# Half of the down projection's width by seven half-size products, in five chunks of the second MLP, with the left operand 64 bytes further on

## The chip, the cores and the metric

The kernel runs on one core of a Trainium2 chip. The metric is the time of one execution on the device in microseconds. The engines are called as in the profile: PE (TensorE, matmuls), PEld (its loads of the stationary operand), DVE (VectorE), ACT (ScalarE), POOL (GpSimd) and SP (SyncE, which issues most DMAs).

## The reference, cut to what matters

The network has two layers over 512 tokens of width 1024. Each layer is a mixer with a normalization and then this MLP with hidden width 4096, also with a residual and a normalization. All is float32.

```python
def sq_relu_mlp(h, w_up, w_down):
    return jnp.square(jax.nn.relu(h @ w_up)) @ w_down

        h = layer_norm(DN_ALPHA * h + sq_relu_mlp(h, mlp_w_up[layer], mlp_w_down[layer]),
                       ln_g[layer, 1], ln_b[layer, 1])
```

## The kernel before

**Three passes.** Each float32 operand is split into a high part (a cast to the matmul type, on ACT) and a low part (the raw value minus the high part, on DVE). A product is high x high, high x low and low x high, so three matmuls for each block of 128 of the contraction. `split` and `wload` do this: they write `wh`/`wl` (weights), `w2h`/`w2l` (half as large), and `hidden` writes `hh`/`hl`.

**Chunks.** `mlp` goes through the hidden width in eight chunks of 512. A chunk's hidden values lie in `hh` and `hl` (128 partitions, four blocks of 512 tokens). The loop over `c` has two halves, `n = 0, 1`. A half computes two blocks of the hidden values of chunk `c + 1` and then one half of the output columns of chunk `c`: `down(c, t, n, ...)` for four tiles `t` of 128 tokens. A `down` is 12 matmuls: left (stationary) operand `hh` or `hl`, moving operand `wh` or `wl` with 512 columns. `V.tensor_tensor` then adds the result from PSUM (`dn`) to the residual `res`.

**The up products.** The two blocks of hidden values are not made by eight half-size products but by seven (Winograd's form): `Pair.m1, m6, m2, m7, m5, m4, m3`, in this order on PE, 12 matmuls of 256 columns each. Their operands are sums of weight blocks, made by POOL (`up_load`: four sums into `sa` and `sb`) and split afterwards, and sums of activations (`TH`, `TL`). Results gather in three PSUM tiles: `a` (m1, m2), `b` (m6, m7, m4) and `d` (m5, m3). Between two products of one tile DVE reads it: `u2` after m6, `u3` after m7, `r22` after m5, so m7 waits for `u2`, m4 for `u3` and m3 for `r22`. `close` applies relu and square on ACT and splits into `hh` and `hl`.

**What sets the order.** Each engine runs its own list of instructions in order; a scheduler builds the lists from the program, and `behind(x, y)` puts x after y. The next pair of up weights is loaded while the current one is used. Raw weights take turns in four buffers (`wr`), `wh` and `wl` in five; a load waits until all readers of its buffer are done. `x0`, `pad2` and the like only set where the tiles lie in memory. `load_gb` loads a normalization's gain and bias.

## Time and profile before

| | |
|---|---|
| median of three runs | 1158.22 us (1158.12 to 1160.28) |
| the profiled execution | 1157.95 us |
| its span in the profile | 1156.2 us |
| busy: PE, DVE, ACT, POOL | 98%, 71%, 48%, 21% |
| DMA | 114.10 MB, mean 99 GB/s |

The profile shows one execution. Its span runs from the first to the last instruction, the execution's time holds 1.75 us more. A PE that is busy by the profile need not run at its peak, since the ends of matmuls are modelled; how far it is ahead is better read from the start times of successive matmuls.

### The profile page before, as it was taken

How to read it: one execution, taken by the hardware profiler on the slowest of the kernel's cores; microseconds unless marked ns; L12 is line 12 of the kernel's file. 1: busy time of each engine (PE TensorE's matmuls, PEld its weight loads, DVE VectorE, ACT ScalarE, POOL GpSimd, SP SyncE). 2: the span in 40 equal slices, each digit the busy share in tenths (PEclk: the TensorE clock that was granted, in tenths of full speed). 3: DMA queues.
4: the chain of work that ended last, by engine and by line, in shares of the span. 5: the costliest groups of instructions: out<-in, count | busy, mean ns of one | idle time of the engine just before them, and what ended most of it. 6: DMA issues, size and time to landing. Idle time of an engine off the chain costs nothing.

```text
span 1156.2 us, 19018 instructions
## 1 busy us (share of the span) xinstructions
PE 1135.4 (98%) x7542; PEld 1004.3 (87%) x7542; DVE 816.6 (71%) x1501; ACT 555.1 (48%) x1015; POOL 244.5 (21%) x177
## 2 busy tenths in 40 slices
PE   9999999999999999999999999999999999999997
PEld 9878789998998898998988887777988898989986
DVE  6667789667887676665665977877976665666657
ACT  6454743465584444444443345542644444444531
POOL 1112120011013242423420200000042422424203
PEclk9999999899999999999999999999999999999999
DMA  8522131304313243332334232202332332323312
GB/s 297 163 75 78 46 90 70 102 19 148 114 68 128 92 128 96 109 106 91 110 105 128 67 104 73 74 1 73 111 127 95 103 114 92 110 96 108 107 55 73
DMA packets 41257, 114.10 MB, mean 99 GB/s; under 512 B 11536, under 2 KB 12304, under 8 KB 41168
## 3 DMA queue, kind: packets, MB, share of 16 engines
q1 hardware_dynamic: 40736, 112.10, 29.7%
q8 instruction: 59, 0.97, 0.3%
q10 hardware_dynamic: 432, 0.79, 0.2%
q14 instruction: 30, 0.25, 0.1%
HBM read 109.46 MB, written 3.41 MB: 98 GB/s over the span
## 4 chain that ended last, share of the span: by engine, by line
PE 87%; DVE 6%; issue 3%; ACT 2%; POOL 1%; DMA 1%; SPq 0%; DVEq 0%; ACTq 0%; POOLq 0%
PE dn L69 30%; PE upb L69 9%; PE upd L69 6%; PE wo L69 6%; PE upa L69 6%; PE up L69 4%; PE projqMM L69 4%; PE kq L69 4%; PE proj_zMM L69 3%; PE v L69 3%; PE ssc L69 1%; PE ov L69 1%; PE ropeMM L69 1%; PE KM L69 1%; PE VM L69 1%
## 5 line engine op out<-in xcount | busy, mean ns | idle before, releaser
L108 ACT CAST wh<-wr 128x1024 fp32r<-128x1024 f32 (+1 forms) x124 | 130.5, 1053 | 213.8 <-PE dn L69 154.8
L109 DVE TENSOR_TENSOR wl<-wr,wh 128x1024 fp32r<-128x1024 f32 (+1 forms) x124 | 169.3, 1366 | 70.1 <-ACT wh L108 69.9
L69 PE MATMUL dn<-wh,hh 128*128 128x512 f32 (+1 forms) x516 | 200.2, 388 | 0.0
L69 PE MATMUL dn<-wh,hl 128*128 128x512 f32 (+1 forms) x516 | 200.1, 388 | 0.0
L69 PE MATMUL dn<-wl,hh 128*128 128x512 f32 (+1 forms) x516 | 200.1, 388 | 0.0
L1149 DVE TENSOR_TENSOR res<-res,dn 128x512 f32<-128x512 f32 (+1 forms) x121 | 82.1, 678 | 64.4 <-PE dn L69 64.3
L69 PEld LDWEIGHTS dn<-wh,hl 128*128 128x128 f32 x516 | 96.9, 188 | 19.9
L1058 POOL TENSOR_TENSOR sa<-wr 128x512 f32<-128x512 f32 x26 | 37.6, 1447 | 359.5 <-DMA wr<-in_up_dram 339.2
L69 PEld LDWEIGHTS dn<-wh,hh 128*128 128x128 f32 x516 | 96.9, 188 | 18.9
L69 PEld LDWEIGHTS dn<-wl,hh 128*128 128x128 f32 x516 | 96.9, 188 | 18.9
L825 POOL TENSOR_TENSOR rs<-rs,nhalf 128x1 f32<-128x1 f32 x16 | 13.2, 824 | 296.1 <-DVE rs L824 250.3
L69 PE MATMUL upb<-TH,wh 128*128 128x256 f32 x216 | 60.5, 280 | 0.7 <-DVE u L1107 0.6
L69 PE MATMUL upd<-XH,wh 128*128 128x256 f32 x216 | 59.9, 277 | 0.4 <-DVE r L1122 0.4
L69 PE MATMUL upa<-XL,wh 128*128 128x256 f32 x216 | 59.9, 277 | 0.0
L69 PE MATMUL upd<-XL,wh 128*128 128x256 f32 x216 | 59.8, 277 | 0.0
L69 PE MATMUL upa<-XH,wl 128*128 128x256 f32 x216 | 59.7, 277 | 0.0
L69 PE MATMUL upd<-XH,wl 128*128 128x256 f32 x216 | 59.7, 277 | 0.0
L69 PE MATMUL upb<-TH,wl 128*128 128x256 f32 x216 | 59.7, 276 | 0.0
L69 PE MATMUL upb<-TL,wh 128*128 128x256 f32 x216 | 59.7, 276 | 0.0
L1060 POOL TENSOR_TENSOR sa<-wr,wr 128x512 f32<-128x512 f32 x26 | 57.2, 2200 | 0.0
L1059 POOL TENSOR_TENSOR sb<-sa,wr 128x512 f32<-128x512 f32 x26 | 54.7, 2104 | 0.0
L975 ACT CAST wh<-wr 128x1024 fp32r<-128x1024 f32 x27 | 28.5, 1054 | 53.6 <-PE upa L69 53.6
(425 smaller groups left out, 3247.0 us busy)
## 6 DMA issues: line engine op xcount, KB each, us to landing
wr<-in_up_dram SPq DMA_DIRECT2D x64, 512.0 KB, 3.7
wr<-in_dn_dram SPq DMA_DIRECT2D x64, 512.0 KB, 3.8
wr<-in_wo_dram SPq DMA_DIRECT2D x16, 512.0 KB, 4.4
wr<-in_bw_dram SPq DMA_DIRECT2D x8, 512.0 KB, 4.2
wr<-in_wk_dram SPq DMA_DIRECT2D x6, 512.0 KB, 4.3
wr<-in_wq_dram SPq DMA_DIRECT2D x6, 512.0 KB, 3.5
wr<-in_wv_dram SPq DMA_DIRECT2D x6, 512.0 KB, 3.7
wr<-in_wz_dram SPq DMA_DIRECT2D x4, 520.0 KB, 3.9
```

The source lines that it names most:

```text
L69: return self.note(nc.tensor.matmul(*args, **kw))
L108: behind(A.copy(hi, raw), first_act)
L109: behind(V.tensor_sub(lo, raw, fr(hi)), first)
L825: G.tensor_tensor(rs, rs, nhalf[:, 0:1], op=ALU.pow)
L975: behind(A.copy(hi, raw), first_act)
L1058: e.tensor_tensor(sa[:, 0], raw[1][:, kA], raw[1][:, kB], op=ALU.add)
L1059: e.tensor_tensor(sb[:, 0], sa[:, 0], raw[0][:, kA], op=ALU.subtract)
L1060: e.tensor_tensor(sa[:, 1], raw[0][:, kA], raw[1][:, kA], op=ALU.subtract)
L1149: V.tensor_tensor(dst, dst, ps, op=ALU.add)
```

## The change

In chunks 2 to 6 of the second layer's MLP (`SD`) the left half of the output columns (0 to 511) is computed as before, but as two quarters of 256 columns each (`Quarter`). The right half (512 to 1023) is computed by seven products of half size (`Down`): the hidden chunk is cut into two halves of the contraction and two of the tokens, the weight into two halves of the contraction and two quarters of the columns. Four of the seven products take sums of hidden values as their left operand (`Sums`, written over `r` and split into `SH0`, `SL0`, `SH1`, `SL1`), four take sums of weights (`T1`, `T2`, `T3`, `T4`: `R1`'s first half, `R0`'s first half, and `tb`). All sums are made by POOL. Each product is 12 matmuls of 256 columns, and DVE adds each partial result to `res` when its product is done (`dns`, 2 x 256 columns).

In these chunks `hid_tiles` places `hh` and `hl` 16 elements (64 bytes) further on in their buffers. The buffers of the MLP are split up anew: `f4` has three instead of five, `r` has its own three, `tb` and the `S` tiles are new. The three PSUM banks of `mmt` get names, so that products can choose one. The gain and bias of the normalizations are loaded at other places. The evictions and splits of `Pair` get more `behind` conditions in these chunks.

```diff
+    def hid_tiles(dt, off=0):
+        both = (hid_pool[1].tile([P, 2112], dt, tag=n, name=nm(n)) for n in ("hh", "hl"))
+        return [h[:, off:off + 2048].rearrange("p (k t) -> p k t", k=4) for h in both]
...
-            return pool.tile(shape, F32, tag="f4", name=nm(n), bufs=5)
+            return pool.tile(shape, F32, tag="f4", name=nm(n), bufs=3)
+        def rt(shape, n):
+            return pool.tile(shape, F32, tag="r", name=nm(n), bufs=3)
...
-        def new_hid():
-            return hid_tiles(F32R)
+        def new_hid(c):
+            return hid_tiles(F32R, 16 if c in SD else 0)
...
+        SD = range(2, NC - 1) if layer == 1 else ()
+        nA, nB = slice(512, 768), slice(768, 1024)
+        class Quarter:
+            def __init__(self, c, m):
+                self.c, self.m = c, m
+                self.raw = columns(c, 0, m)
...
+            def tile(self, t, hid):
+                (hh, hl), (wh, wl) = hid, self.w
+                ps = smt("dnq")[:, 0:256]
+                for k in range(4):
+                    h, l = (x[:, k, t * P:(t + 1) * P] for x in hid)
+                    T.matmul(ps, h, wh[:, k, :], start=k == 0, stop=False)
+                    T.matmul(ps, h, wl[:, k, :], start=False, stop=False)
+                    T.matmul(ps, l, wh[:, k, :], start=False, stop=k == 3)
+                dst = res[:, t, self.m * 256:self.m * 256 + 256]
+                return V.tensor_tensor(dst, dst, ps, op=ALU.add)
+        def columns(c, n, m):
+            raw = wpool[0].tile([P, 4, 256], F32, tag="wr", name=nm("wr"), bufs=wpool[1])
+            for i in range(2):
+                SY.dma_start(raw[:, 2 * i:2 * i + 2, :], dn[layer, c, n, i][:, :, m * 256:m * 256 + 256])
+            return raw
+        class Down:
+            def __init__(self, c):
+                self.R0, self.R1 = (columns(c, 1, m) for m in range(2))
+                self.tb = tb("tb")
+            def sums(self, first):
+                b11, b21, b12, b22 = (r[:, i:i + 2, :] for r in (self.R0, self.R1) for i in (0, 2))
+                t3 = self.tb[:, 0:2, :]
+                behind(G.tensor_tensor(t3, b22, b12, op=ALU.subtract), first)
+                G.tensor_tensor(b12, b12, b11, op=ALU.subtract)
...
+                for rw, cl in zip(rows, cols):
+                    dst = res[:, rw.start // P:rw.stop // P, cl]
+                    self.out = V.tensor_tensor(dst, dst, ps, op=ALU.add)
+            def m1(self):
+                self.a = self.open(0)
+                self.product(self.a, self.hid, 0, tA, self.B11, True, False, [tA], [nA])
...
+        class Sums:
+            def __init__(self, r0, r1):
+                self.r = r0, r1
+                a11, a21, a12, a22 = (r[:, :, t] for r in self.r for t in (tA, tB))
+                G.tensor_tensor(a22, a21, a22, op=ALU.add)
+                G.tensor_tensor(a21, a11, a21, op=ALU.subtract)
+                G.tensor_tensor(a11, a22, a11, op=ALU.subtract)
+                self.last = G.tensor_tensor(a12, a12, a11, op=ALU.subtract)
...
+                    if fast and n == 0:
+                        d.split_0(p.u3_in, p.m2_out)
+                        d.sums_2()
...
+                elif n == 0:
+                    d.sums_3(nxt.sums)
+                    q.tile(0, hid)
+                    d.m1()
+                    nxt.split0(d.out, p.last)
+                    q.tile(1, hid)
+                    d.m2()
+                    nxt.split_b(d.out, p.last)
+                    o = q.tile(2, hid)
+                    d.m6()
+                    nxt.split_a(o, p.last)
+                    q.tile(3, hid)
+                    q = Quarter(c, 1)
+                else:
+                    d.m5()
...
-            if c == 1:
-                gb1 = load_gb(2 * layer + 1)
+            if c == NC - 2:
+                gb1 = load_gb(2 * layer + 1, *(f4([P, D], n) for n in ("lng", "lnb")))
```

How the lists move, at three places. First DVE, from the end of chunk 2 into the first half of chunk 3 of the second MLP, before. `wl` from `wr` with line 109 are the down slabs' splits, `dn` the down results; `u2`, `u3` and `r` with `upd` are the reads that m7, m4 and m3 wait for.

```order
L1149 TENSOR_TENSOR res_69<-res_69,dn_1530_10023 128x512
L109 TENSOR_TENSOR wl_1544_10094<-wr_1542_10091,wh_1543_10093 128x1024
L1149 TENSOR_TENSOR res_69<-res_69,dn_1533_10041 128x512
L109 TENSOR_TENSOR wl_1547_10100<-wr_1545_10097,wh_1546_10099 128x1024
L1107 TENSOR_TENSOR u2_1539_10085<-m1_1537_10070,upb_1538_10072 128x256
L1117 TENSOR_TENSOR u3_1549_10129<-m1_1537_10070,upb_1538_10072 128x256
L1122 TENSOR_TENSOR r_1548_10115<-u3_1549_10129,upd_1550_10131 128x256
L976 TENSOR_TENSOR wl_1557_10200<-wr_1551_10175,wh_1556_10199 128x1024
L1126 TENSOR_TENSOR r_1548_10115<-m1_1537_10070,upb_1538_10072 128x256
```

The same place after the change. `dnq` and `dns` are results of a quarter and of a product; `wr_1554` is the quarter, `wr_1555` is `R0`, split once as it was loaded and once (into `w2l`) when it holds T2.

```order
L1254 TENSOR_TENSOR res_69<-res_69,dns_1508_9831 128x2x256
L1120 TENSOR_TENSOR u2_1561_10228<-m1_1559_10213,upb_1560_10215 128x256
L988 TENSOR_TENSOR w2l_1563_10231<-wr_1538_10052,w2h_1562_10230 128x512
L988 TENSOR_TENSOR wl_1565_10235<-wr_1554_10188,wh_1564_10234 128x1024
L1130 TENSOR_TENSOR u3_1567_10264<-m1_1559_10213,upb_1560_10215 128x256
L988 TENSOR_TENSOR wl_1569_10267<-wr_1555_10191,wh_1568_10266 128x1024
L1135 TENSOR_TENSOR r_1566_10250<-u3_1567_10264,upd_1570_10271 128x256
L1293 TENSOR_TENSOR SL0_1574_10290<-r_1494_9733,SH0_1573_10289 128x1024
L988 TENSOR_TENSOR w2l_1572_10286<-wr_1555_10191,w2h_1571_10285 128x512
L1139 TENSOR_TENSOR r_1566_10250<-m1_1559_10213,upb_1560_10215 128x256
```

The splits no longer stand ahead of `u2` but between `u2`, `u3` and `r`, two ahead of `u3` and one ahead of the read that m3 waits for.

Second POOL, over the two pairs' sums around there, before: only `sa` and `sb`.

```order
L1058 TENSOR_TENSOR sa_1522_9981<-wr_1521_9978 128x512
L1060 TENSOR_TENSOR sa_1522_9981<-wr_1520_9977,wr_1521_9978 128x512
L1059 TENSOR_TENSOR sb_1523_9982<-sa_1522_9981,wr_1520_9977 128x512
L1061 TENSOR_TENSOR sb_1523_9982<-wr_1520_9977,sb_1523_9982 128x512
L1058 TENSOR_TENSOR sa_1553_10179<-wr_1552_10176 128x512
```

After: from the pair's sums of chunk 2's second half to those of chunk 3's first. Between them now stand the four sums of hidden values (`r`), two of `Down` (`tb`, and `wr_1556`, which becomes T1) and the one that writes T2 over `wr_1555`.

```order
L1074 TENSOR_TENSOR sb_1540_10056<-wr_1537_10051,sb_1540_10056 128x512
L1285 TENSOR_TENSOR r_1528_9979<-r_1494_9733,r_1528_9979 128x2x256
L1286 TENSOR_TENSOR r_1494_9733<-r_1494_9733 128x2x256
L1287 TENSOR_TENSOR r_1494_9733<-r_1528_9979,r_1494_9733 128x2x256
L1288 TENSOR_TENSOR r_1528_9979<-r_1528_9979,r_1494_9733 128x2x256
L1212 TENSOR_TENSOR tb_1557_10197<-wr_1556_10194 128x512
L1213 TENSOR_TENSOR wr_1556_10194<-wr_1556_10194,wr_1555_10191 128x512
L1217 TENSOR_TENSOR wr_1555_10191<-wr_1556_10194 128x512
L1071 TENSOR_TENSOR sa_1577_10327<-wr_1576_10324 128x512
```

Seven sums stand between the pairs where none stood; an eighth (into `tb`) follows the next pair.

Third PE, in a down tile of chunk 3 before, from the first slab's last block to the second slab's first (`wh` and `wl` moving, `hh` and `hl` left):

```order
L69 MATMUL dn_1564_10239<-wl_1544_10094,hh_1474_9661 128x512
L69 MATMUL dn_1564_10239<-wh_1543_10093,hl_1475_9662 128x512
L69 MATMUL dn_1564_10239<-wh_1546_10099,hh_1474_9661 128x512
L69 MATMUL dn_1564_10239<-wl_1547_10100,hh_1474_9661 128x512
L69 MATMUL dn_1564_10239<-wh_1546_10099,hl_1475_9662 128x512
```

The same chunk after, from the end of a quarter's tile into the first product.

```order
L69 MATMUL dnq_1579_10334<-wl_1565_10235,hh_1480_9669 128x256
L69 MATMUL dnq_1579_10334<-wh_1564_10234,hl_1481_9670 128x256
L69 MATMUL dns_1580_10348<-wh_1568_10266,hh_1480_9669 128x256
L69 MATMUL dns_1580_10348<-wl_1569_10267,hh_1480_9669 128x256
L69 MATMUL dns_1580_10348<-wh_1568_10266,hl_1481_9670 128x256
```

Every down matmul of these chunks is half as wide, and quarters and products take turns.

More of the change, by code (lines that the diff above doesn't have):

```diff
@@ L1043, in x_sums @@
                 split_copy(t, TH[:, i], TL[:, i])
+            for n in ("w2h", "w2l"):
+                pool.tile([P, 4, P], F32R, tag=n, name=nm(n), bufs=2)
             pool.tile([P, 40], F32, tag="pad3", name=nm("pad3"), bufs=1)
             xq["first"] = pool.tile([P, HT], F32R, tag="x0", name=nm("x0"), bufs=1)
-            pool.tile([P, 24], F32, tag="pad4", name=nm("pad4"), bufs=1)
             A.copy(xq["first"], fr(XH[:, 0, tA]))
@@ new lines, in mlp, with split @@
+        class Sums:
[6 more added lines that the diff above has]
+                self.last = G.tensor_tensor(a12, a12, a11, op=ALU.subtract)
+            def split(self, i, first, first_act):
+                hi, lo = (pool.tile([P, 2, 512], F32R, tag=f"S{n}{i}", name=nm(f"S{n}{i}"), bufs=1) for n in "HL")
+                behind(A.copy(hi, self.r[i]), first_act)
+                behind(V.tensor_sub(lo, self.r[i], fr(hi)), first)
+                return hi, lo
@@ L1184, in downs_last @@
             ln_out(*late_out)
+        gbt = [pool.tile([P, 2, 512], F32, tag=f"S{n}0", name=nm("gb"), bufs=1).rearrange("p a b -> p (a b)")
+               for n in "HL"]
+        for n in "HL":
+            pool.tile([P, 2, 512], F32, tag=f"S{n}1", name=nm("gb"), bufs=1)
+        if layer == 0:
+            gb0 = load_gb(0, *gbt)
         hid, nxt = ups_first()
@@ L1188, in mlp @@
         tables = rotary_tables(pool) if layer == 0 else None
+        sums = None
+        rs_ = {}
         for c in range(NC - 1):
-            later = new_hid()
+            later = new_hid(c + 1)
+            fast = c in SD
             for n in range(2):
@@ L1194, in mlp @@
                 early = c == n == 0
+                if fast and n == 0:
+                    q = Quarter(c, 0)
+                    d = Down(c)
+                    d.hid = hid
+                    d.sums(s_.last)
                 if p is None:
@@ L1285, in shared_kv @@
             split_copy(pt[:, 0:P], *[k[:, t * P:(t + 1) * P] for k in kTs])
-        mixTs = [[lt([P, 4, P], f"mix{n}{t}", 1, F32R) for n in "hl"] for t in range(NT)]
         nsink = lt([P, 12], "nsink", 1)
```

164 lines of the change are left out of this document (122 added, 42 removed).

## The prediction

> **What bounds the kernel now.** I read the page first, then the granted clock and the busy times by stretch, then the chain that ended last, and then the timeline of single engines in the second MLP.
>
> ```profile
> span 1156.2 us, 19018 instructions
> ...
> PE 1135.4 (98%) x7542; PEld 1004.3 (87%) x7542; DVE 816.6 (71%) x1501; ACT 555.1 (48%) x1015; POOL 244.5 (21%) x177
> ...
> PE 87%; DVE 6%; issue 3%; ACT 2%; POOL 1%; DMA 1%; SPq 0%; DVEq 0%; ACTq 0%; POOLq 0%
> ```
>
> TensorE (PE) carries 87% of the chain, so only fewer or faster matmuls make the kernel faster, as long as no other engine gets late. The stretches show whether one does in the chunks that change. The first row is one chunk of the second MLP (start and end, its length, then PE, PEld, DVE, ACT and POOL with counts, granted clock, DMA); the second is chunks 2 to 6 together.
>
> ```profile
> 961.14:1002.00 40.86, 40.86 (x265) 37.09 (x264) 25.51 (x32) 18.59 (x22) 14.28 (x8) 1.00 0.32 103
> 920.30:1126.05 205.75, 205.12 (x1321) 185.94 (x1320) 127.34 (x160) 92.42 (x109) 62.62 (x35) 1.00 0.30 98
> ```
>
> PE is busy without a gap, at a granted clock of 1.00. DVE has 15 us of a chunk to spare and POOL 26. The five chunks take 205.75 us where five of the first row would take 204.30, so 1.45 us of stalls lie in them. The chain has the pace of the matmuls, from a later half chunk:
>
> ```profile
> 1004.81 1.36 PE upb L69 x12
> ...
> 1012.97 10.89 PE dn L69 x48
> ```
>
> Twelve 256-wide matmuls take 1.36 us (0.1133 each) and 48 512-wide ones 10.89 (0.2269 each): a matmul of half the width costs exactly half.
>
> **Term 1, the products.** A chunk's down projection is now 96 matmuls 512 wide, 21.78 us. Afterwards its left half is the same work as 96 of 256, and its right half seven products of 12, so 84 of 256: 180 x 0.1133 = 20.40. The gain is one product, 1.36 us a chunk, 6.8 in five. Every one of these matmuls brings a weight load, 180 for 96; the up products have the same ratio, one load for each 256-wide matmul, at 0.1133.
>
> The Trainium skill (TensorE: Matmul & The Clock Gate, Back-to-back issue gap) gives 262 cycles for 256 columns and 518 for 512 at 2.4 GHz, an estimate of 0.1092 and 0.2158 us, a fixed part for each matmul. By it the change would gain 96 x 0.2158 - 180 x 0.1092 = 1.06 us a chunk, 5.3 in all; the trace, where 12 take 1.36 and 48 take 10.89, shows no such part in this stage.
>
> **Term 2, where the left operand lies.** Not every 256-wide matmul has that pace. These are the first and the last of 47 of the rotary projection, and the first and the last of the 24 that end the kernel:
>
> ```profile
> 656.51 0.37 PE L69 MATMUL ropeMM<-wh,XH 128*128 128x256 f32 x1
> ...
> 662.01 0.28 PE L69 MATMUL ropeMM<-wl,XH 128*128 128x256 f32 x1
> ...
> 1145.10 0.28 PE L69 MATMUL dn<-wh,hh 128*128 128x256 f32 x1
> ...
> 1147.85 0.28 PE L69 MATMUL dn<-wh,hl 128*128 128x256 f32 x1
> ```
>
> 5.50 us over 46 steps and 2.75 over 23 are 0.1196 both. In the built programs the next left operand starts, modulo 256 bytes, 0 bytes past the moving one in that last tile, 192 in the rotary projection, and 64 in the up products at 0.1133. The change puts the hidden tiles at 64, so I give their 132 matmuls a chunk the up products' pace (bounds 0 to 132 x 0.0063 = 0.83 us). The tiles of sums (SH, SL), left operand of four products, lie at 192: 48 x 0.0063 = 0.30 us a chunk (bounds 0 and 0.30). The row with the same distance is the nearest, so I take all of it: 1.5 us in five.
>
> **Term 3, VectorE and GpSimd.** The sums of the operands go to POOL, 16 a chunk instead of 8, and the splits into high and low parts to ACT and DVE. Times from one half chunk, POOL first, then DVE:
>
> ```profile
> 940.65 1.32 POOL L1058 TENSOR_TENSOR sa<-wr 128x512 f32<-128x512 f32 x1 [14.69 <-DMA wr<-in_up_dram]
> 941.93 2.30 POOL L1060 TENSOR_TENSOR sa<-wr,wr 128x512 f32<-128x512 f32 x1
> ```
>
> ```profile
> 941.80 1.25 DVE L109 TENSOR_TENSOR wl<-wr,wh 128x1024 fp32r<-128x1024 f32 x1 [1.76 <-ACT wh L108]
> 942.98 0.68 DVE L1149 TENSOR_TENSOR res<-res,dn 128x512 f32<-128x512 f32 x1
> 943.57 1.74 DVE L109 TENSOR_TENSOR wl<-wr,wh 128x1024 fp32r<-128x1024 f32 x1
> ...
> 949.23 1.22 DVE L976 TENSOR_TENSOR wl<-wr,wh 128x1024 fp32r<-128x1024 f32 x1
> 950.36 0.41 DVE L1126 TENSOR_TENSOR r<-m,upb 128x256 f32<-128x256 f32 x1
> ```
>
> A sum takes 1.32 us (1.28 from start to start). With a DVE split beside it 2.30, about 1.0 more, and the split at 943.57 takes 1.74, since that sum ends at 944.23. The add at 942.98, which reads PSUM, keeps its 0.68. So splits and sums take turns; adds from PSUM do not join. Back to back they alternate, and the one that waits nearly doubles:
>
> ```profile
> 842.87 2.29 POOL L1060 TENSOR_TENSOR sa<-wr,wr 128x512 f32<-128x512 f32 x1
> ```
>
> ```profile
> 841.66 2.34 DVE L976 TENSOR_TENSOR wl<-wr,wh 128x1024 fp32r<-128x1024 f32 x1
> 843.92 1.80 DVE L976 TENSOR_TENSOR w2l<-wr,w2h 128x512 fp32r<-128x512 f32 x1
> ```
>
> The turns of a chunk, before: 12 splits of 1024 at 1.13 (949.23 to 950.36), 2 of 512 at 0.68, 8 sums at 1.28, 25.2 us of 40.86. After: 15 at 1.13 (six for the pairs, two of hidden, two quarters, three of Down, two of Sums), 3 at 0.68, 16 sums at 1.28: 39.5 us. The matmuls of the chunk then take 40.86 - 1.36 = 39.5. **The turns fill the chunk**, and what counts is where they run late.
>
> ```profile
> L976 DVE TENSOR_TENSOR w2l<-wr,w2h 128x512 fp32r<-128x512 f32 x2 | 1.4, 684 | 0.0
> ```
>
> DVE itself has room: 19.0 us of splits, 18 adds of 256 at 0.41 and 7 of 512 at 0.68 make 31.1 of 39.5.
>
> Time zero of the walk is the end of a chunk's second row of up products. Rows for it, PE and then DVE:
>
> ```profile
> 951.57 10.89 PE dn L69 x48
> ```
>
> ```profile
> 955.50 1.22 DVE L983 TENSOR_TENSOR hl<-r,hh 128x1024 fp32r<-128x1024 f32 x1 [0.47 <-ACT hh L982]
> ```
>
> The split of the hidden part (hl) ends 955.50 + 1.22 - 951.57 = 5.15 us after zero; it now meets the next pair's last sum, 1.0 more, 6.15. Only then may Sums overwrite r. POOL's queue holds six sums from there (four of Sums, two of Down), 7.7 us, and DVE's five splits in turn with them (A11/A12, sb, sa, A22, quarter) push them by 4 x 1.0 + 0.6: they end at 18.45. The down products of that half take 8 x 1.36 = 10.88, so this is 7.6 into the next half. The split of R0, behind it, ends at 8.7 and the add of r22 behind that at 9.1. Product m3 writes the bank that r22 reads, and is due after six products, at 8.16. I take **0.9 us in chunks 3 to 6**, 3.6 in all; chunk 2 follows a chunk without these sums. Bounds: 0, if hl goes first, and 2.0, with one more exchange of 1.0. Behind r22 wait the splits of SL0 and T2, two adds and the evictions, which have the whole down part (9.5 us) as cover.
>
> **Term 4, an old stall.** One wait of this kind is in the trace, at the start of chunk 2:
>
> ```profile
> 920.23 0.31 DVE wl L109
> ...
> 924.73 0.42 DVE u L1107
> ...
> 925.19 1.68 PE upb L69 x12
> 926.87 1.41 PE upd L69 x12
> ```
>
> Two slab splits wait for sums, the add of u2 behind them comes late, and PE waits. In the new order no slab split stands ahead of u2, so I count 1.3 of the 1.45 us as gained (bounds 0 and 1.45).
>
> **At nothing.** DMAs of the down weights double in number for the same bytes; a tile lands 3.8 us after its issue (row below), R1, the last, some 3 us ahead of its first sum by the walk, and with that cover gone a load costs up to those 3.8 us. The gain and bias loads pass SP's queue elsewhere; in the second MLP they land over 20 us ahead of the last normalization. In the first up products of both layers other splits change places while DVE is full (27.99 of 28.00 us): bounds -1 and +1.
>
> ```profile
> wr<-in_dn_dram SPq DMA_DIRECT2D x64, 512.0 KB, 3.8
> ```
>
> ```profile
> 820.00:848.00 28.00, 27.89 (x195) 25.47 (x194) 27.99 (x30) 18.57 (x34) 7.01 (x4) 1.00 0.44 141
> ```
>
> **The sum.** -6.8 + 1.5 + 3.6 - 1.3 = -3.0 us. The profiled execution took 1157.95 (its span 1156.2 and 1.75 around it), so 1154.95; the median of the runs is 0.27 higher, so **1155.2**. A measurement of this kernel tells about 0.2%, 2.3 us, from no change.
>
> **Rivals.**
> - *The turns fit.* hl goes ahead of the pair's sums and r22 is in time. For it: DVE's 8.4 us to spare. Against: the sum of turns, 39.5 of 39.5. Without term 3: 1151.6.
> - *The backlog grows.* After the late r22 the adds behind SL0 and T2 end about 3.1 us after the first half's up products, hl about 7.3 after, and then come two splits, two adds and a sum of POOL: the split of sb ends 11.6 after, where m6 of the next half is due at 9.52 + 1.36 = 10.9. 0.7 more in four chunks: 1158.0, no change.
> - *The pace does not recover* (slower). After the wait at 925 each product took 1.41 us instead of 1.36, until the 512-wide matmuls. The new chunks have none, so from the first wait in chunk 3 on all 348 matmuls could run at 0.1175: 348 x 0.0042 x 4 = 5.8 us, 1161.0. Against: other 256-wide products kept 1.36.
> - *The 64 bytes do nothing*, and the hidden tiles run at the last tile's 0.1196: 0.83 x 5 = 4.2 us, 1159.4.
>
> **How the numbers follow.** Forecast 0.36 (own range 1153 to 1157.5), turns fit 0.17, backlog 0.20, pace 0.17, no use of the 64 bytes 0.10. Faster than 1155.9: two thirds of the forecast, all of the second, a little of the third, 0.44. Slower than 1160.5: the fourth and the edges of the third and fifth, 0.22. The rest, 0.34, lies between. The range, 1150.8 to 1161.5, takes in the second and the fourth and the bounds of terms 2 and 3 that they hold.
>
> **What would show it.** Chunks 2 to 6 should take 202.7 us. Term 1 and 2: 1.36 us for a quarter's 12 matmuls or a product of the hidden tiles, 1.43 for one of the sums. Term 3: PE waits of about 0.9 for the add of r22 in chunks 3 to 6 and none for u2 in chunk 2, with splits of 1.7 to 2.3 us and sums of 2.3 there. Waits for the split of sb instead mean the backlog; 1.41 everywhere, the pace. A PE wait at u3, on a DMA, or outside these chunks would make the working wrong.

## The result, and the profile after

| | before | after |
|---|---|---|
| median of the runs | 1158.17 us (1155.54 to 1160.28) | 1171.6 us (1169.38 to 1172.44) |
| span of the profiled execution | 1156.2 us | 1170.7 us |

The changed kernel is slower: the ratio is 1.0114, with an interval of 1.0089 to 1.0139. The forecast was 1155.2, and the range ended at 1161.5.

First the page of the changed kernel: the span, the busy times, the chain that ended last, and the landing of the weights.

```profile
span 1170.7 us, 20012 instructions
...
PE 1139.0 (97%) x7962; PEld 1022.4 (87%) x7962; DVE 875.3 (75%) x1556; ACT 567.3 (48%) x1035; POOL 314.8 (27%) x217
...
PE 77%; DVE 10%; issue 6%; ACT 4%; POOL 2%; DMA 1%; SPq 0%; DVEq 0%; POOLq 0%; ACTq 0%
...
wr<-in_up_dram SPq DMA_DIRECT2D x64, 512.0 KB, 3.3
```

PE's share of the chain fell from 87% to 77%, and DVE's rose from 6% to 10%. To see where, I took from both timelines the start of the first matmul of each stage; the differences of these starts are the stage's length.

| stage, from first matmul to first matmul | before | after | difference |
|---|---|---|---|
| all up to the first layer's first pair | 341.82 | 340.05 | -1.8 |
| first layer's MLP, first to last half with a pair | 267.77 | 275.54 | **+7.8** |
| second layer, rotary to query projection | 13.95 | 19.22 | **+5.3** |
| second layer's MLP, long up products to the second half | 45.18 | 47.81 | **+2.6** |
| its chunks 2 to 6 | 205.75 | 206.63 | **+0.9** |

The five changed chunks are 0.9 longer, where 3.05 less was forecast. The other 15.7 us lie in stages whose products the change does not touch. Three mechanisms carry them. The -1.8 of the first row fits the granted clock: around 220 us it is 0.50 for 13.65 us in the profile before and for 10.24 in the one after, and 3.41 us at half the clock are 1.7 us of PE's time, by an estimate. It lies between 10.24 and 17.07 us in the profiles of all kernels here.

**The first layer.** The waits of PE between 345 and 640 us, after (who waits for whom: us in total, times, longest):

```profile
PE upb L69 <- DVE u L1120: 4.9, 9, 0.6
PE upd L69 <- DVE XL L1357: 0.6, 1, 0.6
PE upd L69 <- DVE r L1135: 0.4, 1, 0.4
```

Before, that view has one wait of 0.4 in all, for r22. Nine times PE now waits for the add of u2. (The wait for `XL`, in the first pair, is also in the profiles of experiments 2 and 17, which are the kernel before with one small edit each, at 0.5 us.) One such half in the timelines of POOL, DVE and PE (start, duration):

```profile
466.23 1.31 POOL L1071 TENSOR_TENSOR sa<-wr 128x512 f32<-128x512 f32 x1 [12.91 <-DMA wr<-in_up_dram]
467.50 1.33 POOL L1073 TENSOR_TENSOR sa<-wr,wr 128x512 f32<-128x512 f32 x1
...
467.55 2.36 DVE L115 TENSOR_TENSOR wl<-wr,wh 128x1024 fp32r<-128x1024 f32 x1 [1.76 <-ACT wh L114]
469.83 0.67 DVE L1162 TENSOR_TENSOR res<-res,dn 128x512 f32<-128x512 f32 x1
470.43 1.71 DVE L115 TENSOR_TENSOR wl<-wr,wh 128x1024 fp32r<-128x1024 f32 x1
472.07 0.41 DVE L1120 TENSOR_TENSOR u<-m,upb 128x256 f32<-128x256 f32 x1
...
472.53 0.39 PE L69 MATMUL upb<-TH,wh 128*128 128x256 f32 x1 [0.65 <-DVE u L1120]
```

and the same half before:

```profile
464.60 1.32 POOL L1058 TENSOR_TENSOR sa<-wr 128x512 f32<-128x512 f32 x1 [12.01 <-DMA wr<-in_up_dram]
465.87 2.31 POOL L1060 TENSOR_TENSOR sa<-wr,wr 128x512 f32<-128x512 f32 x1
...
465.71 1.29 DVE L109 TENSOR_TENSOR wl<-wr,wh 128x1024 fp32r<-128x1024 f32 x1 [1.76 <-ACT wh L108]
```

The order is decided by a few hundredths of a microsecond. The first slab split starts 0.07 to 0.08 ahead of the half's first product in both (467.62 and 465.79). Before, it starts 0.16 ahead of POOL's second sum, so the sum waits (2.31). After, the sum starts 0.05 ahead of the split, so the split waits (2.36), everything behind it on DVE is 1 us later, and u2 is late. The sums come earlier because a pair's weights land earlier: in this half the second load is issued 4.85 us ahead of the first product in both, and lands after 3.33 us instead of 3.53. Over the first layer's MLP the medians are 3.25 and 3.70 us.

**The start of the second layer.** DMA issues of SP after (start, time of the issue):

```profile
670.20 0.33 SPq L1457 DMA_DIRECT2D pm<-kv  x1
```

before:

```profile
654.32 0.33 SPq L1254 DMA_DIRECT2D pm<-kv  x1
```

This load is 15.9 us later, 10 more than PE's own delay there. It follows the last normalization's instructions on `res` (L895, SP's waits after show 2.3 us for it). The change put that normalization's gain and bias into `f4` buffers of the first MLP's pool, so the pool's memory, of which `pm` gets a part, is only free when the last row is normalized. The cast and the split of `pm` on ACT and DVE are late by that:

```profile
673.47 0.62 ACT L155 CAST KMh<-pm 128x512 fp32r<-128x512 f32 x1 [1.61 <-DMA pm<-kv]
```

```profile
674.12 0.69 DVE L156 TENSOR_TENSOR KMl<-pm,KMh 128x512 fp32r<-128x512 f32 x1 [0.72 <-ACT KMh L155]
```

PE's stop comes before them and does not wait for `pm`. It waits until DVE has read an earlier result of the rotary projection (`rp`, DVE, then PE):

```profile
673.12 0.28 DVE L1472 TENSOR_TENSOR rp<-ropeMM,sinT 128x128 f32<-128x128 f32 x1
```

```profile
673.55 0.55 PE L69 MATMUL ropeMM<-wh,XH 128*128 128x256 f32 x1 [2.64 <-DVE rp L1472]
```

`rp` is a tile of the same new pool, and DVE comes to it behind the last row's normalization, which ends at 670.14, and the splits after it. The trace shows this order, but not whether the memory or the scheduler's list sets it; experiment 4 changes both.

The stop costs more than itself. At 672.7 us the granted clock falls to 0.50 for 6.83 us. The rotary projection ahead of the stop and behind it, with the columns of the prediction's stretches (the clock is the third number from the end):

```profile
660.08:670.91 10.83, 10.83 (x89) 10.22 (x87) 10.71 (x17) 2.86 (x5) 1.67 (x4) 1.00 0.36 124
673.55:679.30 5.75, 5.75 (x28) 5.75 (x28) 3.88 (x14) 2.12 (x4) 0.00 (x0) 0.50 0.89 290
```

Behind the stop 24 matmuls of the projection step 0.213 us instead of 0.118, an estimate of 24 x 0.095 = 2.3 us. With the stop of 2.64 that is most of the 5.3. Experiments 1, 3, 8 and 16 have the same stop, then 3.41 us at a clock of 0.50, and the stage takes 18.15 to 18.58; without the stop no profile has a lower clock there.

**The second MLP's first chunk.** POOL, then ACT:

```profile
845.91 9.92 POOL L1071 TENSOR_TENSOR sa<-wr 128x512 f32<-128x512 f32 x1 [14.80 <-DMA wr<-in_up_dram]
```

```profile
859.76 1.05 ACT L987 CAST wh<-sb 128x1024 fp32r<-128x1024 f32 x1 [7.83 <-POOL sb L1074]
860.72 0.59 ACT L1030 ACTIVATE relu<-up 128x512 f32<-128x512 f32 x1
```

A sum that takes 1.3 us alone was held for 8.6 us by a row of DVE instructions that followed each other without a gap. That alone costs nothing (experiment 8). But the scheduler now places the cast of `sb` ahead of the hidden part's relu on ACT. The cast waits 7.83 us for the sums, the relu behind it is late, and PE stops twice in the down products (1.4 for `res`, 0.6 for `relu` by its waits).

**The five chunks** themselves, as in the prediction's rows of before (length, then PE, PEld, DVE, ACT, POOL), and PE's waits there:

```profile
934.36:1140.99 206.63, 204.18 (x1741) 202.00 (x1740) 179.45 (x216) 107.87 (x130) 122.50 (x72) 1.00 0.32 105
```

```profile
PE upb L69 <- DVE u L1130: 1.3, 2, 0.7
PE upd L69 <- DVE r L1135: 0.7, 2, 0.4
PE upb L69 <- DVE wl L988: 0.3, 1, 0.3
```

1740 matmuls at 0.1133 are 197.2 us, so 9.4 are lost. Of the 145 products of 12 matmuls, 66 are slow: they run at 0.118 a matmul instead of 0.113 (in all counts below, slow is a median step above 0.1155). 66 x 12 x 0.0044 = 3.5. The other 5.9 are steps longer than that, so PE stands; the view of waits counts less of them, since it begins at the modelled end of the matmul before. No wait for u2 is left at the start of chunk 2.

### The profile page after: what moved, and what is told of

It is laid out like the page before. It is cut to its first block, busy times and chain, and to the rows that moved or that the text cites. A ratio compares the mean times of both kernels' runs of the same rounds, so it can differ in the third digit from the quotient of the medians.

```text
span 1170.7 us, 20012 instructions
## 1 busy us (share of the span) xinstructions
PE 1139.0 (97%) x7962; PEld 1022.4 (87%) x7962; DVE 875.3 (75%) x1556; ACT 567.3 (48%) x1035; POOL 314.8 (27%) x217
## 3 DMA queue, kind: packets, MB, share of 16 engines
HBM read 109.46 MB, written 3.41 MB: 96 GB/s over the span
## 4 chain that ended last, share of the span: by engine, by line
PE 77%; DVE 10%; issue 6%; ACT 4%; POOL 2%; DMA 1%; SPq 0%; DVEq 0%; POOLq 0%; ACTq 0%
PE dn L69 19%; PE upb L69 8%; PE upd L69 6%; PE wo L69 5%; PE upa L69 4%; PE projqMM L69 4%; PE dnq L69 4%; PE kq L69 4%; PE dns L69 3%; PE proj_zMM L69 3%; PE v L69 3%; PE up L69 2%; DVE wl L115 2%; PE ssc L69 1%; PE ov L69 1%
## 5 line engine op out<-in xcount | busy, mean ns | idle before, releaser
L115 DVE TENSOR_TENSOR wl<-wr,wh 128x1024 fp32r<-128x1024 f32 (+1 forms) x104 | 146.2, 1407 | 49.3 <-ACT wh L114 48.7
L69 PE MATMUL dn<-wh,hh 128*128 128x512 f32 (+1 forms) x356 | 138.2, 388 | 1.9 <-DVE res L1160 1.4
L69 PE MATMUL dn<-wh,hl 128*128 128x512 f32 (+1 forms) x356 | 137.9, 387 | 0.0
L69 PE MATMUL dn<-wl,hh 128*128 128x512 f32 (+1 forms) x356 | 137.8, 387 | 0.0
L1162 DVE TENSOR_TENSOR res<-res,dn 128x512 f32<-128x512 f32 (+1 forms) x81 | 54.7, 675 | 41.3 <-PE dn L69 41.2
L69 PEld LDWEIGHTS dn<-wh,hh 128*128 128x128 f32 x356 | 66.9, 188 | 15.8 <-DVE res L1160 1.8
L69 PEld LDWEIGHTS dn<-wh,hl 128*128 128x128 f32 x356 | 66.8, 188 | 13.7
L69 PEld LDWEIGHTS dn<-wl,hh 128*128 128x128 f32 x356 | 66.9, 188 | 12.8
L988 DVE TENSOR_TENSOR wl<-wr,wh 128x1024 fp32r<-128x1024 f32 x47 | 69.5, 1479 | 0.0
L995 DVE TENSOR_TENSOR hl<-r,hh 128x1024 fp32r<-128x1024 f32 x27 | 34.2, 1265 | 24.8 <-ACT hh L994 24.8
```

Of the source, the lines that this page charges most:

```text
L69: return self.note(nc.tensor.matmul(*args, **kw))
L115: behind(V.tensor_sub(lo, raw, fr(hi)), first)
L988: behind(V.tensor_sub(lo, raw, fr(hi)), first)
L995: V.tensor_sub(hl, r, fr(hh))
L1162: V.tensor_tensor(dst, dst, ps, op=ALU.add)
```

## The experiments

Theory: the loss lies outside the chunks, in the three mechanisms; inside, the seven products give back what they save to a pace of 0.118 and to waits for VectorE. Rival: the seven products lose the time. All lengths below come from start times as in the table above. Ratios are against the kernel before, run on the same chip.

**1. The old products, with the rearrangement kept.**

```diff
-        SD = range(2, NC - 1) if layer == 1 else ()
+        SD = ()
```

> The changed kernel with the list of chunks that use the seven products empty: all chunks have the old down products, and only the rearrangement of buffers, gains and loads is left. Theory (the loss lies outside the five chunks: 7.0 us in the first layer's MLP, 5 at the start of the second layer, 2.6 in its first chunk; the five chunks themselves came out 0.9 us longer): 1158.2 + 7 + 5 + 2.6 = about 1172, slower than before, and within 2 us of the changed kernel. Rival (the seven products lose the time): back at 1158.

1164.04 us, ratio 1.0055 (1.0039 to 1.0071): between the two theories. The second layer's start (18.16) and the first chunk (46.73) lose 4.2 and 1.6 of their 5.3 and 2.6, but the first layer takes 268.77, with one wait for u2 of 0.2. The pairs' weights land in 3.7 us here: without the early landing the meeting of sums and splits makes u2 late only once. So the first layer's loss does hang on the seven products being in the program, though not on running them.

**2. The address shift alone.** The change also makes a scratch area smaller, which moves the tiles in memory. This is the kernel before, with that line alone:

```diff
-    nc = bacc.Bacc("TRN2", target_bir_lowering=False, num_devices=1)
+    nc = bacc.Bacc("TRN2", target_bir_lowering=False, num_devices=1, dynamic_dma_scratch_size=256)
```

> The kernel before with only the smaller scratch area, which moves every tile of SBUF's left side down by 16128 bytes. In the changed kernel the weights of a pair land in 3.3 us instead of 3.7, and by that GpSimd's sums meet the slab splits. If the shift or the scratch area makes the loads faster: landing 3.3 us, and 3 to 7 us more in the first layer's MLP, 1161 to 1165. If the faster landing comes from elsewhere: 1158, landing 3.7.

1156.92 us, ratio 1.0 (0.9989 to 1.001), landing 3.7. The shift does nothing to the time or to the landing.

**3. The sums wait for the slab split.**

```diff
+            hold(e.tensor_tensor(sa[:, 0], raw[1][:, kA], raw[1][:, kB], op=ALU.add), held)
...
+            hold(e.tensor_tensor(sa[:, 1], raw[0][:, kA], raw[1][:, kA], op=ALU.subtract), held)
...
+                    nxt = Pair(f0, held=None if fast or p is None else wlast[0])
```

`hold` is a dependency with a semaphore; `wlast` is the last slab split.

> The changed kernel, with GpSimd's first two sums of a pair made to wait for the half's second slab split wherever the down products are the old ones. Theory (in the first layer a sum that starts just ahead of the first slab split makes that split last 2.1 to 2.4 us, the add of u2 comes late, and PE waits 0.6 to 0.8 us in ten halves): those waits go, first layer's MLP 7 us shorter, total 1164.5. Rival (it is the 1.41 us pace or the loads that cost the time there): within 2 us of the changed kernel, 1170 to 1173.

1162.76 us, ratio 1.0039 (1.0024 to 1.0054). The first layer takes 266.62, 1.15 less than before the change. The same half, POOL and DVE:

```profile
469.89 1.32 POOL L1080 TENSOR_TENSOR sa<-wr 128x512 f32<-128x512 f32 x1 [15.19 <-DVE wl L116]
```

```profile
466.85 1.23 DVE L116 TENSOR_TENSOR wl<-wr,wh 128x1024 fp32r<-128x1024 f32 x1 [1.76 <-ACT wh L115]
467.99 0.68 DVE L1171 TENSOR_TENSOR res<-res,dn 128x512 f32<-128x512 f32 x1
468.59 1.22 DVE L116 TENSOR_TENSOR wl<-wr,wh 128x1024 fp32r<-128x1024 f32 x1
```

Both splits are back at 1.23 and 1.22, and the weights still land in 3.2 us: the meeting is the cause, the landing only its occasion.

**4. A pool of their own for the gains.** The pool stays open until the second MLP; both loads of the first MLP and that of the second mixer use it.

```diff
+    gpool = gstack.enter_context(tc.tile_pool(name="gbp", bufs=1))
+    def own_gb():
+        return [gpool.tile([P, D], F32, tag=n, name=nm(n), bufs=1) for n in ("lng", "lnb")]
...
-            gb0 = load_gb(0, *gbt)
+            gb0 = load_gb(0, *own_gb())
...
-                gb1 = load_gb(2 * layer + 1, *(f4([P, D], n) for n in ("lng", "lnb")))
+                gb1 = load_gb(2 * layer + 1, *(own_gb() if layer == 0 else (f4([P, D], n) for n in ("lng", "lnb"))))
...
-        gb0 = load_gb(2, *gbt)
+        gb0 = load_gb(2, *own_gb())
```

> The changed kernel, with the gains and biases of the first layer's MLP and of the second layer's mixer in two tiles of a pool of their own, as before the change, instead of buffers of the MLP's pool. Theory (the first tile of the second layer's pool takes memory of the MLP's pool, so its load waits for the last normalization, which reads its gain there, and all loads behind it on SP's queue wait too: 670.2 instead of 654.3): the load starts some 14 us earlier relative to the end of the down products, PE's gap ahead of the query projection goes, 5 us less, 1166.6. Rival (the order of the splits on VectorE there costs the time): no change, 1170 to 1173.

1169.46 us, ratio 1.0099 (1.0082 to 1.0116), only 2.1 less than the changed kernel. The stage itself went from 19.22 to 13.68, all of its 5.3. The profile has the stages ahead of the first pair 1.9 longer (341.98 against 340.05), with the clock at 0.50 there for 13.65 us instead of 10.24. The load of `pm` is now issued at 632.82 us, PE's wait of 2.64 for `rp` is gone, and so is the stretch at half the clock.

**5 and 6. All three repairs, with the seven products and with the old ones.** To the edits of experiments 3 and 4 comes the order on ACT (`hcopy` is the hidden part's last cast); the sixth has `SD = ()` as well.

```diff
-                        nxt.split_b()
+                        nxt.split_b(None, xq["hcopy"] if layer == 1 and p is None else None)
```

> The changed kernel with three repairs outside the five chunks: GpSimd's first two sums wait for the second slab split where the down products are old, the gains have a pool of their own, and in the second layer's first chunk ScalarE casts the first pair's sums (sb) only after the hidden part of the last long up products. Theory (the loss outside is 7.8 + 5.3 + 2.6, and the five chunks are 0.9 us longer): 1171.6 - 15.7 = 1156, within 0.3% of the kernel before. Rival (there are other losses, or the repairs cost as much elsewhere): above 1160.

1156.66 us, ratio 0.9993 (0.9983 to 1.0004).

> The three repairs, and the old down products in all chunks: against the run with the three repairs alone this is the price of the five changed chunks by themselves. By the forecast of the prediction the seven products gain 3.0 us, so this run is 3 us longer than that one, 1159. By the traces (five chunks 206.6 us, against 205.0 with the old products and without the late add) it is 1 to 2 us shorter: 1154 to 1155.

1153.72 us, ratio 0.9967 (0.9955 to 0.998). The first three stages are equal in both (266.6, 13.69, 45.2). Chunks 2 to 6 take 206.01 with the seven products and 204.51 with the old ones. So the loss outside is explained, and the seven products cost 1.5 us by the profiles and 2.9 by the medians. (In the sixth, the sums are held in chunks 2 to 6 as well.) Terms 1 to 3 of the prediction make them a gain of 1.7 (term 4, the old stall, is gone in both).

**7. The kernel before, with the sums held in all halves.** `hold` as in experiment 3, and

```diff
-                    nxt = Pair(f0)
+                    nxt = Pair(f0, held=None if p is None else wlast[0])
```

> The kernel before, with GpSimd's first two sums of a pair made to wait for the second slab split in all halves. If the meeting of sums and slab splits is what makes the add of u2 late, the wait of 0.8 at 924 us and the slow products behind it go (1.3 us), and the spread of the runs narrows: 1156 to 1157. If the waiting sums come late themselves for the next pair's splits: above 1160.

1154.7 us, ratio 0.9975 (0.9966 to 0.9984): this version and the sixth beat both kernels. Chunks 2 to 6 take 204.51, 1.24 less, and the first layer gains 1.16, so the old stall at 925 us was of the same kind. But without any hold experiment 2 has no PE wait in these chunks either (204.67), and 268.70 in its first layer: which halves lose the turn differs between kernels that are nearly alike, and each was profiled once.

**8. The order on ACT alone.** The changed kernel with only the edit shown under 5.

> The changed kernel with only the order on ScalarE in the second layer's first chunk changed: the cast of sb behind the hidden part. Theory (that cast waits 7.8 us for GpSimd's sums and holds the hidden part's relu, square and cast behind it, so the down products stop twice, 1.1 and 1.9 us): the two stops go, the way from the second layer's long up products to its second half is 45.2 us as before instead of 47.8. Rival (GpSimd's sum of 9.9 us is itself the cause, and the next products wait for its split instead): a wait of 2 us appears at the first product with sb.

1169.58 us in one run. The long up products to the second half take 45.20, as before, with POOL's sum as long as it was (10.01):

```profile
845.87 10.01 POOL L1071 TENSOR_TENSOR sa<-wr 128x512 f32<-128x512 f32 x1 [14.72 <-DMA wr<-in_up_dram]
```

So the order cost the 2.6 us, not the long sum.

**9 and 10. Two other places of left operands**, with the three repairs. In 10 a second pad behind the `S` tiles keeps all later tiles at their place modulo 256.

```diff
-            return hid_tiles(F32R, 16 if c in SD else 0)
+            return hid_tiles(F32R, 0)
```

```diff
+            pool.tile([P, 32], F32, tag="pad5", name=nm("pad5"), bufs=1)
             for i in range(2):
                 for n in "HL":
                     pool.tile([P, 2, 512], F32, tag=f"S{n}{i}", name=nm("gb"), bufs=1)
+            pool.tile([P, 32], F32, tag="pad6", name=nm("pad6"), bufs=1)
```

> The three repairs, and the hidden tiles at offset 0 in the five chunks too, instead of 64 bytes further on. Theory place (each matmul whose left operand lies at the wrong distance takes 0.118 instead of 0.113): the 132 matmuls a chunk with hidden tiles go to 0.118, those that are slow already stay, 1.5 to 3 us longer, 1158 to 1160. Theory state (PE is in a slow or a fast state, and the quarters are where it comes back to the fast one): slow nearly throughout the five chunks, 3 to 4 us longer, 1160. Rival (64 bytes do nothing): 1156.7.

> The three repairs, and the tiles of sums (SH, SL) 128 bytes further on, so that they lie like the up products' operands. By term 2 of the prediction the products with sums then gain 0.3 us a chunk, 1.5 in all, 1155.2. Rival, from the trace of the changed kernel (three of their four products run at 0.1133 where the quarters beside them do, and at 0.118 where those do): no change, 1156.7, and slow stretches at the same places.

With the hidden tiles at 0: 1159.07 us, ratio 1.0013 (1.0001 to 1.0025), five chunks 208.10, 98 of 145 products slow. 55 of these have a third pace, 0.120: all eight quarters of a chunk and all three products with hidden tiles. One down part, where the products of sums between the quarters keep the fast pace:

```profile
1118.22 1.36 PE dns L69 x12
1119.58 1.44 PE dnq L69 x12
1121.02 1.36 PE dns L69 x12
1122.38 1.44 PE dnq L69 x12
```

So the 64 bytes do something: without them all 55 run at 0.120, with them some run at 0.118 and the rest at 0.1133. With the sums at 64: 1157.97 us, ratio 1.0002 (0.9992 to 1.0012), five chunks 207.85, 121 of 145 slow, which neither reading forecast. So places matter by about 2 us in the profiles, but term 2 has the sums the wrong way round: at 64 all products of the second half's down part are slow, at 192 nearly all are fast. With sums at 192 (fifth run) the quarter behind the product m6 or m5 is fast in all ten down parts; at 64 it is slow in all ten.

**11. R0's split behind r22**, with the three repairs.

```diff
-                        d.split_0(p.u3_in, p.m2_out)
-                        d.sums_2()
                     p.m5()
...
+                        d.split_0(p.r22, p.m2_out)
+                        d.sums_2()
                         d.split_t2(p.r22, p.m2_out)
```

> The three repairs, and on VectorE and ScalarE the split of R0 (with GpSimd's difference that overwrites R0) behind the add of r22 instead of behind that of u3. Theory of term 3 (that split waits for GpSimd's difference and holds r22 back, so product m3 waits 0.5 in chunks 3 to 6): those four waits go, 2.1 us, and the first left products are still in time: 1154.6. Rival (the turns are full, so the lateness moves on): a wait of 0.5 to 1 at the first product with R0, or at m6 of the next half, and 1156 to 1158.

1158.28 us, ratio 1.0 (0.9988 to 1.0012), five chunks 207.71. PE's waits there in the fifth run and in this one:

```profile
PE upd L69 <- DVE r L1144: 1.1, 3, 0.4
PE upb L69 <- DVE u L1139: 0.6, 1, 0.6
```

```profile
PE upb L69 <- DVE wl L997: 2.1, 5, 0.4
PE upb L69 <- DVE u L1139: 0.6, 1, 0.6
```

The waits for r22 went, and five for the split of sb came: the lateness moved on.

**12 and 13. The first right operand of m1** in halves behind 256-wide down products: from XH itself (12, where the line has `None` for the copy), or from a second copy at another place (13).

```diff
-                product(self.a, self.A11, xq["B11"], True, False, xq["first"])
+                product(self.a, self.A11, xq["B11"], True, False, xq["again" if self.again else "first"])
...
+                xq["again"] = pool.tile([P, HT], F32R, tag="x1", name=nm("x1"), bufs=1)
...
+                A.copy(xq["again"], fr(XH[:, 0, tA]))
```

> The three repairs; in the halves that follow 256-wide down products the first matmul of m1 reads its right operand from XH itself and not from the small copy. In the trace the slow pace (0.118) begins at m1 in nearly all of these halves. If the copy's place starts it there: halves stay at 0.1133, 2 to 3 us less, 1154. Rival (it is the change from 256-wide down products to the up products, or the waits): no change, 1156.7.

> The three repairs; in the halves that follow 256-wide down products the first matmul of m1 reads its right operand from a second copy that lies 192 bytes (modulo 256) ahead of the next left operand, instead of 96. Theory (a step of 192 followed by steps of 64 brings PE back to the fast pace): the up products of these nine halves run at 0.1133 from m1 on, some 30 of the 66 slow products go, 30 x 12 x 0.0044 = 1.6 us, unless VectorE is the later for it: 1155. Rival (the slow pace comes from the waits or from the change between kinds of products): the same map of slow products, 1156.7.

1156.82 us (0.9987, 0.9972 to 1.0002) and 1156.28 us (0.9985, 0.9968 to 1.0001): no change, with 71 and 67 slow products (67 in the fifth run), and the slow stretches begin at m1 as there. The copy does not start the slow pace, and the step of 192 does not end it there.

**14 and 15. Without POOL's sums of the hidden part**, alone and with the copy of 13.

```diff
-                G.tensor_tensor(a22, a21, a22, op=ALU.add)
-                G.tensor_tensor(a21, a11, a21, op=ALU.subtract)
-                G.tensor_tensor(a11, a22, a11, op=ALU.subtract)
-                self.last = G.tensor_tensor(a12, a12, a11, op=ALU.subtract)
+                self.last = None
```

> The three repairs; GpSimd's four sums of the hidden part are left out, so the four products that use them compute with unsummed tiles; 12 sums a chunk instead of 16, and all else is the same. Theory of term 3 (splits and sums take turns, 39.5 us of 39.5 in a chunk, so something is always late): 5.1 us of turns a chunk less, no PE wait above 0.3 in the chunks, 2.3 us less, 1154.3. Rival (the order on VectorE makes the waits, not the load): the waits for r22 stay at 0.5 in chunks 3 to 6, 1156.7.

> The two edits together: the second copy at a step of 192, and GpSimd's sums of the hidden part left out. If pace and turns are the whole of it, the five chunks come to the 197.2 us of their matmuls plus the six slow down products a chunk that stay, 1.6: 199 us instead of 206.1, 1150. If something else holds them, above 1153.

1151.51 us, ratio 0.9941 (0.992 to 0.9963), and 1151.17 us, ratio 0.9942 (0.9922 to 0.9962). The stretch of the five chunks in 14:

```profile
918.09:1121.00 202.91, 202.91 (x1744) 202.61 (x1743) 171.43 (x216) 108.24 (x130) 86.24 (x54) 1.00 0.32 107
```

PE is busy in all of it, and the view of its waits is empty; the window reaches 0.58 us past the five chunks, which take 202.33. So the 20 sums of hidden values, of some 72 instructions of POOL, bring all of the waits of the fifth run. This fits full turns, and 1151.51 is even less than the 1154.3 of that theory. But without the sums the splits of `S` also need not wait for them, and the run does not separate the two. What is left over 197.2 is mostly the slow pace (87 of 145 products slow in 14; 62 in 15, five chunks 200.93).

**16 and 17. What brings the early landing.** The seven products in chunk 6 alone (of the changed kernel), and the kernel before with small loads of the second layer's down slabs in chunks 2 to 6:

```diff
-        SD = range(2, NC - 1) if layer == 1 else ()
+        SD = (6,) if layer == 1 else ()
```

```diff
-        SY.dma_start(raw, src)
+        if halves:
+            SY.dma_start(raw[:, :, 0:256], src[:, :, 0:256])
+            SY.dma_start(raw[:, :, 256:512], src[:, :, 256:512])
+        else:
+            SY.dma_start(raw, src)
```

> The changed kernel with the seven products in chunk 6 alone. If the landing in the first layer goes with the number of small loads or of instructions: between 3.3 and 3.7 us, and some of the ten waits for the add of u2 remain. If any use of the seven products brings it: 3.3, ten waits, 7 to 8 us lost in the first layer, about 1171. If it is 3.7: one or two waits, 1164 as with the old products.

> The kernel before, with each slab of the down weights of chunks 2 to 6 of the second layer loaded by two DMAs of half the columns (256 KB, lines of 1 KB), as the changed kernel loads its quarters. If these loads are what makes the pairs' weights land earlier in the first layer: 3.3 us there, ten waits of 0.6 to 0.8, about 1165. If it is the length of the program or its place in memory: 3.7 and 1158.

16: 1176.79 us, more than any of its three readings forecast, landing 3.3, seven waits for u2 in the first layer and nine more in chunks of the second, whose down products are the old ones there. 17: 1156.96 us, ratio 0.9995 (0.9983 to 1.0006), landing 3.6. The small loads are not it. In the first layer's MLP every profiled program with the seven products, 13 of 13 on several chips, has 3.2 to 3.3; the six without have 3.6 to 3.7. What in the program does it stays open.

## Why the prediction was wrong

- **What failed: what the prediction put at nothing.** Its sum takes every stage outside the five chunks as unchanged. "At nothing" gives side edits bounds of -1 and +1 ("other splits change places while DVE is full") for the first up products alone, and the gain and bias loads nothing. The runs showed 7.8, 5.3 and 2.6 us instead. In the first layer POOL's sums take the turn ahead of the slab split, and u2 is late (removed by experiment 3). At the start of the second layer the gains hold back the next pool, PE stops for 2.64 us, and then it runs at half the clock (experiment 4). In the second MLP's first chunk the cast of `sb` stands ahead of relu on ACT (experiment 8); only this one lies where bounds were given. The 7.8 are no effect of the side edits alone, since experiment 1 keeps them and loses 1.0 there. They come with the seven products, through loads that land earlier, and the prediction took the landing as it was. What moves the landing stays open. The prediction does end on the sign of such a loss ("A PE wait at u3, on a DMA, or outside these chunks would make the working wrong"), but no rival has a price for it. Part of the rows was at hand: term 3 shows that splits and sums exclude each other, and in the trace of before the half at 465.79 was 0.16 us from losing the turn.
- **The gains.** The prediction says that the loads of the second MLP come early enough, which held. It does not ask what the buffer that now holds the gain keeps from being free. Experiment 4 shows that it was the next pool, its first load among it.
- **Term 1** held in its size: a product of 12 takes 1.36 where PE is at its fast pace. No run reaches the 197.2 us of all products at that pace; the nearest is 200.93, in experiment 15, which leaves the sums out.
- **Term 2** was right for place 0 and wrong for the rest. Its row of the rotary projection is misread: the 0.1196 there averages one first step of 0.205 us with 45 of 0.118. The last tile's steps are 0.120 throughout, and that place costs the same in experiment 9. So the rival "The 64 bytes do nothing" is out; the five chunks lose 2.1 us without them, not its 4.2, since many of the same products are slow at 64 too. At 64 and at 192 the place of a product's own operands does not set its pace: products with sums at 192 run at 0.1133 in the second halves, the quarters at 64 run at 0.118 in the first. What ran before does: behind a product of sums at 192 PE is fast, behind one at 64 it stays slow (experiment 10). The excess over the fast pace is 3.5, not 1.5. It resembles the rival "the pace does not recover" (5.8), but PE comes back without 512-wide products, and the slow stretches stay in experiment 14, which has no waits. What starts the slow pace, 12 and 13 do not find.
- **Term 3** named a mechanism that the runs bear out, though experiment 14 does not show it alone, and was too small: 5.9 us of waits, not 3.6. The add of r22 is late by 0.5 in two chunks (three in the fifth run), not by 0.9 in four. The add of u3 is late by 0.8 in two others, and the split of sb by 0.2 to 0.5 in four: the backlog that was a rival of its own comes on top. In experiment 11 the lateness moves from one place to another, as one shortage would.
- **Term 4** came true in part by luck: no wait for u2 is left at the start of chunk 2, but experiments 2 and 17, which keep the old order, do not have it either (204.67 and 205.30). The 1.3 us were read from one profile. Experiment 7 gains as much with a single order.

## What to carry to other kernels

A change that touches a shared pool, a buffer count or a scheduler's input has to be priced at every place that depends on it, above all where two engines reach for the same turn within 0.2 us of each other: such a place cost next to nothing here until something else moved it, and one ordering dependency takes the chance out of it (0.25% for the kernel before, by itself). When tiles move into another pool, ask who gets that memory next and what now has to end first. Before trading matmuls for sums, add up the turns of the engines that make the sums: at 39.5 of 39.5 us a saved 1.36 us on PE was not cashed here. And price a stop of PE with the clock that follows it: 2.64 us cost some 2.3 more.

## What the runs showed of the hardware that was not expected

- The turn does not always alternate. Back to back, splits and sums took 2.3 us each by the prediction's rows; but a sum behind a row of DVE instructions that all were ready took 9.92 us (10.01 in experiment 8). The Trainium skill (SBUF — State Buffer, SBUF: two separate sides) says that whoever starts first gets the pair of ports for the whole instruction and the other blocks fully; the 2.36 and 2.31 at one and the same place agree, and the 9.92 shows that the blocked one need not come next.
- PE has three paces for 256-wide matmuls with a weight load each at a granted clock of 1.00: 0.1133, 0.118 and 0.120 us. The 0.120 goes with the place of the left operand (experiment 9). Between the other two PE keeps one over many products. In the fifth run it goes slow at m1 of every half that follows 256-wide down products, and comes back behind a product of sums at 192 or after a wait. Why is open: an empty list of waits (14) leaves it, and so do other places of m1's first right operand (12, 13).
- In the five profiles with a PE stop of 2.64 us in the rotary projection, the granted clock falls to 0.50 within 1.8 to 4.7 us of the last matmul before it, partly when PE is back at work, for 3.41 us in four and 6.83 in one. In all 19 profiles each stretch at 0.50 ahead of the kernel's last products is a multiple of 3.41 us long (up to 17.07).
- The landing of the same 512 KB loads, issued at the same point of the same half, differs by 0.4 us between programs that differ only hundreds of microseconds later.
